# Pairs with one quarter in seven products: another order of quarters and products, another source for the second bank's copy, and a later start of the embedding weights

## The chip, the cores and the metric

The kernel runs on one core of a Trainium2 chip, as one program launched once. The metric is the time of one execution in microseconds (us) on the device. Engines are named as the profile names them: PE is TensorE (matmuls), DVE is VectorE, ACT is ScalarE, POOL is GpSimd, and SP is the queue that issues most loads. Each engine works through its own list of instructions in order; semaphores hold one engine back until another, or a DMA, is done.

## The reference, cut to what matters

The model is a trunk of two layers over 256 tokens of width 2048, each with a large input projection, a token mixer, a gate and an output projection; after the mixers stands a gated embedding of 256 inputs per layer. What the change touches are projections of width 2048 by 2048 and the product of the embedding with its weights, so only their forms matter:

```
# even layer: m is the mixers' output; odd layer the same with other weights
h   = h + m @ W_o                     # W_o: 2048 x 2048, stages "eo" and "oo"
# gated per-layer embedding
e   = rmsnorm(p @ W_p) * row          # row: one weight per feature, 2048
h   = h + sigmoid(h @ W_g) * e        # W_g: 2048 x 2048, stages "g0" and "g1"
# the odd layer's large projections, stages "oog", "oz" and others
y   = rmsnorm(h) @ W
```

The output is the whole trunk, 256 by 2048, in fp32.

## The kernel before

**Tiles.** A projection of 2048 features into 2048 is cut into four chunks of 512 output features. A chunk has four quarters: 512 of the 2048 input features each. The weights of a quarter are two tiles of 128x1024 in fp32. Every tile goes the same way: SP loads it (`raw`, five buffers), ACT rounds it to fp32r (`whi`, a CAST), DVE subtracts to get the rest (`wlo`), and PE multiplies tokens (also in a high and a low part, `ahl`) by high, low, high. A plain quarter has 24 matmuls of 128x512: 12 into the bank of the first 128 tokens, then 12 into the bank of the second. `whi` and `wlo` have four buffers each, so the CAST of a tile waits until PE has finished with the tile four before it. The PSUM banks come from pools of three (`mm`), three (`mx`) and two (`st`).

**Stages.** In `eo`, `g0` and `oo` the first two chunks are done plainly, eight quarters in the order of a list in `project_two`; then `seven` does the last two chunks as a pair. `seven` is also called by the odd layer's projections `oog` and `oz`. In a pair, some of the four quarters (`kqs`) are done for both chunks at once by a scheme with seven products (numbered 1 to 7, as in Strassen's method) in place of eight. A product has six matmuls per quarter. Four pairs have one quarter in seven products: those of `eo`, `g0` and `oo`, and the first of `oog`. Three pairs (in `oog` and `oz`) have two.

**Banks of a pair.** A and F hold the first chunk's two halves of tokens, E and B the second's. Product 1 goes into A; then ACT copies A to F and, with the sign turned, A to B (lines 334 and 335). Products 5, 6 and 7 are added up in B, 2 in A, 4 in F, and the other one into E. After 5 and after 6 ACT keeps a copy of B in SBUF (`keep`, line 316); after 7 DVE subtracts B from the copy kept after 5. The remaining quarters are plain: the first chunk's into A and F (call them a), the second's into E and B (call them b). Sums of weight tiles (line 304) are made by DVE in the tiles `ch` and `raw` in place.

**Consumers.** `seven` is a generator: it yields a finished half chunk, and its caller queues what follows. In `eo` and `oo` that is `out_proj`: DVE adds the bank to the residual (line 586, `hq`), transposes it in blocks (549, `w`), and sends it to DRAM and back in another layout (`across`), where it returns as `r`; ACT and DVE split `r` into the next stage's `ahl`. In `g0` it is `ple_gate`: a tanh, a product with the embedding `pl`, a sum into `hq`, and then the same way round (`to_features`, line 557 for the scaled reading of `r` on ACT). Steps of such work are run by `pump`, which is called between the two halves of a plain quarter and at some places of `seven`. Where an instruction lands in its engine's list is then set by a scheduler: weight CASTs and subtractions, copies of banks and the like have raised priorities.

**Embedding weights.** `row` (line 529) loads two tiles of 128x1024 by two DMAs that POOL issues (line 533), one row of weights spread over all partitions; `ple_gain` (line 537) multiplies the eight tiles `pl` by them on DVE (line 541), in eight steps that `pump` runs. They are started when the first half chunk of `eo` is handed out, and drained when `eo` is through.

**Names.** In the orders below a number behind a name tells one buffer from another: in the pair of `eo`, bank A is `mm_3425`, F `mm_3426`, B `mm_3427` and E `mx_3424` before, and A `mm_3421`, F `mm_3422`, B `mm_3423` and E `mx_3420` after.

Of the kernel before, what the change touches and what calls it, by code (L numbers as in the profile page):

```python
# [15 lines left out]
AF = mybir.ActivationFunctionType  # L16
ALU = mybir.AluOpType
# [5 lines left out]
KT = D // P  # L23
EPS = 1e-6
RSQRT_MAGIC = 0x5F3759DF


_PRM = [
# [15 lines left out]
def trunk(ctx: ExitStack, tc: tile.TileContext, a, out):  # L44
    nc = tc.nc
    v, s, gp, te, sy = nc.vector, nc.scalar, nc.gpsimd, nc.tensor, nc.sync
# [17 lines left out]
    def start(lane, gen):  # L64
        lanes.setdefault(lane, []).append(gen)
# [9 lines left out]
    def pump():  # L75
        with ExitStack() as behind:
            for ins in last.values():
                behind.enter_context(tc.issue_after(ins))
            for lane in list(lanes):
                step(lane)  # L80

    def drain(*which):
        for lane in which:
            while step(lane):
                pass
# [135 lines left out]
    def product(o, stat, parts, first=False, end=False):  # L221

        n = 2 * len(parts)
        for k in range(n):
            xh, xl = (x[k] for x in stat)
            wh, wl = (x[:, (k % 2) * 512:(k % 2 + 1) * 512] for x in parts[k // 2])
            for i, (x, y) in enumerate(((xh, wh), (xh, wl), (xl, wh))):
                with ExitStack() as behind:
                    if k + i == 0:
                        behind.enter_context(tc.issue_after(last["pe"]))  # L230
                    last["pe"] = te.matmul(o, x, y, start=(first and k + i == 0), stop=(end and k == n - 1 and i == 2),  # L231
                                           skip_group_check=True).ins
# [4 lines left out]
    def plain(w, j, kq, act, ps, first=(False, False), end=False):  # L237

        parts = load_weights(w[4 * j + kq])
        for hf in range(2):  # L240
            product(ps[hf], stationary(act, (2 * kq, 2 * kq + 1), hf), parts, first[hf], end)
            if hf == 0:
                pump()
# [35 lines left out]
        keep(d, (2, 4))  # L279
        yield  # L280

    def seven(w, j, act, qs, kqs, room, part, home=None):

        def src(b, side, kq):
            return block(w[4 * (j + b) + kq], side * 1024, 1024)

        def load(tile_of, b, side):
            tiles = []
            for kq in kqs:
                t = tile_of()  # L290
                sy.dma_start(out=t, in_=src(b, side, kq))
                tiles.append(t)
            return tiles

        def ring():
            return wp.tile([P, 1024], F32, name="raw", tag="raw", bufs=5)

        def split(tiles):
            return [split_weights(t) for t in tiles]

        def add(x, y):
            with tc.high_priority(offset=400):
                for xi, yi in zip(x, y):
                    v.tensor_tensor(out=xi, in0=xi, in1=yi, op=ALU.add)

        def add_loaded(x):
            for xi, kq in zip(x, kqs):
                gp.dma_start(out=xi, in_=src(1, 0, kq), accum_op=ALU.add)

        def soon(out, in0, in1, op):  # L310
            with tc.high_priority(offset=450):
                v.tensor_tensor(out=out, in0=in0, in1=in1, op=op)

        def keep(out, bank):
            with tc.high_priority(offset=450):
                s.copy(out, bank)

        def quadrant(side, hf):
            return stationary(act, [2 * kq + side for kq in kqs], hf)

        def combo(n):
            return [[t for kq in kqs for t in qs[n, kq][x]] for x in range(2)]

        two = len(kqs) == 2
        rest = [kq for kq in range(4) if kq not in kqs]
        E = px.tile([P, 512], F32, name="mx", tag="mx")
        A, F, B = (pm.tile([P, 512], F32, name="mm", tag="mm") for _ in range(3))
        b5, g = part(), part()
        X = load(room, 0, 0)
        product(A, quadrant(0, 0), split(X), True)  # L330
        if two:
            add_loaded(X)
        with tc.high_priority(offset=450):
            s.copy(F, A)
            s.activation(B, A, AF.Copy, scale=-1.0)  # L335
            if home is not None:
                s.copy(E, home)
        Y = load(room, 1, 1)
        product(E, combo(4), split(Y), home is None)
        if not two:  # L340
            W = load(ring, 1, 0)
            add(Y, W)
            add(W, X)
        plain(w, j, rest[0], act, (A, F))
        product(B, combo(1), split(X if two else W))
        add(X, Y)
        if two:
            add_loaded(Y)
        keep(b5, B)
        if not two:  # L350
            plain(w, j, rest[1], act, (A, F))
            product(B, combo(2), split(X))
            keep(g, B)
        pump()
        Z = load(ring, 0, 1)
        product(A, quadrant(1, 0), split(Z))
        if not two:
            add(X, Z)
        plain(w, j, rest[-1], act, (A, F))
        yield 0, 0, A  # L360
        if two:
            product(B, combo(2), split(X))
            add(X, Z)
            keep(g, B)
            product(F, quadrant(1, 1), split(X), end=True)
            pump()
        product(B, combo(3), split(Y))
        soon(b5, B, b5, ALU.subtract)
        if not two:
            product(F, quadrant(1, 1), split(X), end=True)  # L370
        soon(b5, F, b5, ALU.subtract)
        pump()
        yield 0, 1, b5
        for kq in rest:
            plain(w, j + 1, kq, act, (E, B), end=(kq == 3))
        if home is None:
            soon(g, E, g, ALU.add)
            yield 1, 0, g
        else:
            soon(home, E, g, ALU.add)  # L380
            yield 1, 0, None
        yield 1, 1, B
# [145 lines left out]
    def row(pool, tag, bufs, i):  # L528

        halves = []  # L530
        for b in range(2):
            t = pool.tile([P, 1024], F32, name="row", tag=tag, bufs=bufs)
            gp.dma_start(out=t, in_=a["rows"][i, b * 1024:(b + 1) * 1024].partition_broadcast(P))
            halves.append(t)
        return halves

    def ple_gain(pls, rows):
        yield
        for g in range(4):
            for pl in pls[g]:  # L540
                v.tensor_tensor(out=pl, in0=pl, in1=rows[g // 2][:, (g % 2) * 512:(g % 2 + 1) * 512], op=ALU.mult)
                yield
# [49 lines left out]
    def ple_gate(hq, parts, pls, rp, hss, gain, lane, more):  # L592

        nxt = {}
        for c, hf, src in parts:
            th = tp.tile([P, 512], F32, name="th", tag="th")
            h = hq[c][:, hf]
            s.activation(th, src, AF.Tanh, scale=0.5)
            v.scalar_tensor_tensor(th, th, 1.0, pls[c][hf], op0=ALU.add, op1=ALU.mult)
            v.scalar_tensor_tensor(h, th, rp[:, hf:hf + 1], h, op0=ALU.mult, op1=ALU.add)  # L600
            if not hf:
                continue
            start(f"{lane}{c}", to_features(hq[c], c, nxt, gain, lane, more))
            step(f"{lane}{c}")
            for hf in range(2):
                squared(hq[c][:, hf], hss[:, c, hf:hf + 1])
        return nxt

    def small(n, name, rows=P):
# [8 lines left out]
    pls = embed(a["pw"], None, lambda: p0.tile([P, 512], F32, name="pl", tag="pl"),  # L618
                lambda: sy.dma_start(out=prm, in_=a["prm"]))
# [82 lines left out]
    def gate_tok(w, j, act, u):  # L702
# [7 lines left out]
    mx, e0, e1, lb, omb, sp, ez, z2, pol, sp8, spm8 = (small(8, n) for n in (  # L710
        "mx", "e0", "e1", "lb", "omb", "sp", "ez", "z2", "pol", "sp8", "spm8"))
# [44 lines left out]
    if True:  # L756
        ew = a["ew"]
        fs, qs, ks, xcs = {}, {}, {}, {}
# [339 lines left out]
    def mixed():  # L1098
        for c, hf, src in two_and_seven(a["eo"], y, ready(y, "fm"), (ap, "ahl"), in_e0):
            if hf == 0 and c in (1, 2):  # L1100
                load_hq(c + 1, last["hop"])
            if (c, hf) == (0, 0):
                m0_scope.close()
                pe0.append(l0.enter_context(tc.tile_pool(name="e0", bufs=1)))
                start("pg", ple_gain(pls, row(pe0[0], "row", 2, 0)))
            yield c, hf, src

    def pieces(tile):
# [5 lines left out]

    pe0 = []
    act = out_proj(hq, mixed(), "fe")
    drain("pg")
    e0 = pe0[0]

    gr = e0.tile([P, KT, 16], F32, name="gr")  # L1120
    sy.dma_start(out=gr, in_=a["ogf"])
# [45 lines left out]
    with tc.tile_pool(name="m1", bufs=2) as m1:  # L1167
# [47 lines left out]
        li, xf, ab, Bc, Mx = (t8(n) for n in ("li", "xf", "ab", "Bc", "Mx"))  # L1215
# [465 lines left out]
```

## Time and profile before

| | us |
|---|---|
| median of three runs | 1029.18 |
| lowest and highest of them | 1028.33, 1034.85 |
| the profiled execution, its own time | 1026.88 |
| its span in the trace | 1025.1 |
| PE busy in the span | 1012.5 |
| DVE busy | 823.2 |
| ACT busy | 649.9 |
| POOL busy | 105.5 |
| start of the pair in `eo` | 343.4 |
| start of the pair in `g0` | 429.2 |
| start of the pair with one quarter in `oog` | 661.7 |
| start of the pair in `oo` | 885.2 |

The page of the profile gives busy times over the span; the prediction reads the page's totals and then single stretches of the trace: the waits of an engine, the chain of work that ended last, and each engine's instructions in order of time. A row of such a timeline reads: start, duration, engine, line, operation, out<-in, how many in a row, and in brackets how long the engine had been idle before and what released it. PE's matmuls overlap: one lasts 0.39 us and the next begins 0.23 us after its start.

### The profile page before, as it was taken

Reading aid. Unit: us, or ns where it says so; the run is one execution under the profiler, and the core shown is the slowest. Engines: PE = TensorE matmul, PEld = TensorE weight load, DVE = VectorE, ACT = ScalarE, POOL = GpSimd, SP = SyncE. Lnnn points to the kernel's source line nnn. Section 1 sums busy time; section 2 is a strip of 40 time slices with the busy share of each in tenths; the row PEclk is TensorE's granted clock in tenths of the full one; section 3 lists DMA queues with packets and bytes.
Section 4 is the critical chain, followed back from the end, with each engine's and each line's share of the span. In section 5 each row is a group of like instructions: output and inputs, shape, how many; then the busy total and the mean of one; then the engine's idle time right before and its main releaser. Section 6 shows DMA issues by size and latency. Waiting matters only on the chain.

```text
span 1025.1 us, 14489 instructions
## 1 busy us (share of the span) xinstructions
PE 1012.5 (99%) x5170; PEld 840.3 (82%) x5170; DVE 823.2 (80%) x1208; ACT 649.9 (63%) x933; POOL 105.5 (10%) x190
## 2 busy tenths in 40 slices
PE   9999999999999999999999999999999999999996
PEld 8888888888888888878888888888888888888885
DVE  7858968969686997788559997779889997976783
ACT  7675554686974555576457876766676777554652
POOL 0111101011112121021011100000011111112000
PEclk9999999999999999999999999999999999999999
DMA  9987756567689798579688755377879888689652
GB/s 363 332 248 227 221 176 199 173 199 231 229 262 295 278 313 252 179 262 311 215 293 248 232 184 189 124 229 206 257 191 283 219 285 317 197 266 304 191 184 83
DMA packets 69672, 242.14 MB, mean 236 GB/s; under 512 B 9024, under 2 KB 10432, under 8 KB 69600
## 3 DMA queue, kind: packets, MB, share of 16 engines
q1 hardware_dynamic: 54720, 193.36, 57.0%
q0 software_dynamic: 14448, 47.33, 16.6%
q8 instruction: 40, 0.66, 0.2%
q10 hardware_dynamic: 432, 0.52, 0.1%
q14 instruction: 32, 0.26, 0.1%
HBM read 221.26 MB, written 19.92 MB: 235 GB/s over the span
## 4 chain that ended last, share of the span: by engine, by line
PE 95%; ACT 2%; DVE 1%; issue 1%; DMA 1%; POOL 0%; ACTq 0%
PE mm L231 21%; PE mm L207 17%; PE mm L209 17%; PE mm L208 17%; PE mx L231 6%; PE mx L209 4%; PE mx L208 3%; PE mx L207 3%; PE mm L502 1%; PE mx L502 1%; PE mm L1506 1%; PE mm L1505 1%; PE mm L1507 1%; PE nu L1315 1%; DMA r<-dfg 1%
## 5 line engine op out<-in xcount | busy, mean ns | idle before, releaser
L136 DVE TENSOR_TENSOR wlo<-raw,whi 128x1024 fp32r<-128x1024 f32 (+1 forms) x317 | 381.4, 1213 | 127.7 <-ACT whi L135 119.9
L135 ACT CAST whi<-raw 128x1024 fp32r<-128x1024 f32 (+1 forms) x317 | 331.0, 1048 | 224.8 <-PE mm L209 108.8
L207 PE MATMUL mm<-whi,ahl 128*128 128x512 f32 x768 | 300.2, 391 | 0.0
L208 PE MATMUL mm<-wlo,ahl 128*128 128x512 f32 x768 | 299.0, 389 | 0.0
L209 PE MATMUL mm<-whi,ahl 128*128 128x512 f32 x768 | 298.9, 389 | 0.0
L231 PE MATMUL mm<-whi,ahl 128*128 128x512 f32 x552 | 178.7, 390 | 1.0 <-ACT mm L335 0.9
L207 PEld LDWEIGHTS mm<-whi,ahl 128*128 128x128 f32 x768 | 144.2, 188 | 30.2 <-issue 0.4
L209 PEld LDWEIGHTS mm<-whi,ahl 128*128 128x128 f32 x768 | 144.2, 188 | 30.1
L208 PEld LDWEIGHTS mm<-wlo,ahl 128*128 128x128 f32 x768 | 144.2, 188 | 29.3
L231 PEld LDWEIGHTS mm<-whi,ahl 128*128 128x128 f32 x552 | 103.6, 188 | 24.2 <-ACT mm L335 2.3
L231 PE MATMUL mm<-wlo,ahl 128*128 128x512 f32 x276 | 107.5, 389 | 0.0
L218 DVE TENSOR_TENSOR wlo<-ch,whi 128x1024 fp32r<-128x1024 f32 x56 | 67.5, 1222 | 11.0 <-ACT whi L217 9.4
L217 ACT CAST whi<-ch 128x1024 fp32r<-128x1024 f32 x56 | 58.3, 1052 | 15.2 <-PE mm L231 7.2
L207 PE MATMUL mx<-whi,ahl 128*128 128x512 f32 x160 | 62.2, 389 | 0.0
L208 PE MATMUL mx<-wlo,ahl 128*128 128x512 f32 x160 | 62.2, 389 | 0.0
L209 PE MATMUL mx<-whi,ahl 128*128 128x512 f32 x160 | 62.2, 389 | 0.0
L231 PEld LDWEIGHTS mm<-wlo,ahl 128*128 128x128 f32 x276 | 51.8, 188 | 10.7
L231 PE MATMUL mx<-whi,ahl 128*128 128x512 f32 x144 | 47.3, 389 | 0.0
L231 PE MATMUL mm<-whi,q 128*128 128x512 f32 x120 | 40.5, 390 | 0.0
L208 PEld LDWEIGHTS mx<-wlo,ahl 128*128 128x128 f32 x160 | 30.0, 188 | 6.3
L209 PEld LDWEIGHTS mx<-whi,ahl 128*128 128x128 f32 x160 | 30.0, 188 | 6.2
L207 PEld LDWEIGHTS mx<-whi,ahl 128*128 128x128 f32 x160 | 30.0, 188 | 6.2
(377 smaller groups left out, 1230.7 us busy)
## 6 DMA issues: line engine op xcount, KB each, us to landing
raw<-in_ew_dram SPq DMA_DIRECT2D x64, 512.0 KB, 4.9
raw<-in_g_dram SPq DMA_DIRECT2D x62, 512.0 KB, 4.7
raw<-in_oqk_dram SPq DMA_DIRECT2D x32, 512.0 KB, 4.5
raw<-in_ov_dram SPq DMA_DIRECT2D x32, 512.0 KB, 4.3
raw<-in_eo_dram SPq DMA_DIRECT2D x30, 512.0 KB, 5.3
raw<-in_oo_dram SPq DMA_DIRECT2D x30, 512.0 KB, 5.2
raw<-in_oog_dram SPq DMA_DIRECT2D x24, 512.0 KB, 4.2
raw<-in_oz_dram SPq DMA_DIRECT2D x20, 512.0 KB, 5.1
```

The lines of the kernel that those rows point to most:

```text
L135: last["act"] = s.copy(h, r).ins
L136: last["dve"] = v.tensor_tensor(out=l, in0=r, in1=h.bitcast(F32), op=ALU.subtract).ins
L207: te.matmul(ps[hf], xh, wh, start=(k == 0), stop=False)
L208: te.matmul(ps[hf], xh, wl, start=False, stop=False)
L209: last["pe"] = te.matmul(ps[hf], xl, wh, start=False, stop=(k == KT - 1)).ins
L217: last["act"] = s.copy(hi, r).ins
L218: last["dve"] = v.tensor_tensor(out=lo, in0=r, in1=hi.bitcast(F32), op=ALU.subtract).ins
L231: last["pe"] = te.matmul(o, x, y, start=(first and k + i == 0), stop=(end and k == n - 1 and i == 2), skip_group_check=True).ins
L502: last["pe"] = te.matmul(ps[hf][:, o:o + w_], tokens(pact[x], k, hf), (hi, lo)[y][:, k * 512 + o:k * 512 + o + w_], start=(n == mine[0]), ...
L1315: te.matmul(ps[:, 0:n], x[:, i, o:o + P], y[:, b, i], start=(b == 0 and x is sh and y is vh), stop=(b == hf and y is vl))
L1505: te.matmul(o, xh, wh, start=(k == 0), stop=False)
L1506: te.matmul(o, xh, wl, start=False, stop=False)
```

## The change

It has three parts.

- The order of quarters and products in a pair is now a string of letters. For a pair with one quarter in seven products the order was, in these letters, `a5a6.2aA74.Fbbb`, and is now `a5a6.7b2.4aAFbb` (digits: products; a, b: plain quarters; a point: `pump`; A, F: the half chunk is handed out). So product 7 comes right behind 6, one of the second chunk's quarters comes ahead of 2 and 4, and both halves of the first chunk are handed out together with two quarters left in place of three. Pairs with two quarters keep their order but for the place of a `pump` and of a sum of weight tiles.
- B is copied from F, with the sign turned, and no longer from A.
- The two loads and eight products of the embedding weights are started when `eo` is through, and drained in the loop of `ple_gate`, ahead of the first use.

```diff
+ORDERS = {1: "a5a6.7b2.4aAFbb", 2: "a5.2aA64.7F.bb"}
...
         with tc.high_priority(offset=450):
             s.copy(F, A)
-            s.activation(B, A, AF.Copy, scale=-1.0)
+            s.activation(B, F, AF.Copy, scale=-1.0)
...
-        plain(w, j, rest[0], act, (A, F))
-        product(B, combo(1), split(X if two else W))
-        add(X, Y)
...
-        if not two:
-            plain(w, j, rest[1], act, (A, F))
-            product(B, combo(2), split(X))
-            keep(g, B)
-        pump()
-        Z = load(ring, 0, 1)
-        product(A, quadrant(1, 0), split(Z))
...
+        rows = [list(rest), list(rest)]
+        did = set()
+        for op in order or ORDERS[len(kqs)]:
+            if op in "ab":
+                b = "ab".index(op)
+                kq = rows[b].pop(0)
+                plain(w, j + b, kq, act, ((A, F), (E, B))[b], end=not rows[b])
...
+            elif op == "6":
+                product(B, combo(2), split(X))
+                keep(g, B)
...
+            elif op == "7":
+                product(B, combo(3), split(Y))
+                soon(b5, B, b5, ALU.subtract)
...
         for c, hf, src in parts:
+            drain("pg")
             th = tp.tile([P, 512], F32, name="th", tag="th")
...
-                start("pg", ple_gain(pls, row(pe0[0], "row", 2, 0)))
...
-    drain("pg")
     e0 = pe0[0]
+    start("pg", ple_gain(pls, row(e0, "row", 2, 0)))
```

Three places of the engines' lists show what it moves. The first is PE in the pair of `eo`, from the start of product 6; `q4` are the combined tokens of a product, `ahl` plain tokens. Before, product 6 goes into bank B and then product 2 into bank A:

```order
L231 MATMUL mm_3427<-whi_3544,q4_3148 128x512 [waits Activation_49]
L231 MATMUL mm_3427<-wlo_3545,q4_3148 128x512 [waits DVE_49]
L231 MATMUL mm_3427<-whi_3544,q4_3148 128x512 x2
L231 MATMUL mm_3427<-wlo_3545,q4_3148 128x512
L231 MATMUL mm_3427<-whi_3544,q4_3148 128x512
L231 MATMUL mm_3425<-whi_3558,ahl_2791 128x512 [waits Activation_49]
L231 MATMUL mm_3425<-wlo_3559,ahl_2791 128x512 [waits DVE_49]
```

After, in the same place:

```order
L232 MATMUL mm_3423<-whi_3538,q4_3148 128x512 [waits Activation_49]
L232 MATMUL mm_3423<-wlo_3539,q4_3148 128x512 [waits DVE_49]
L232 MATMUL mm_3423<-whi_3538,q4_3148 128x512 x2
L232 MATMUL mm_3423<-wlo_3539,q4_3148 128x512
L232 MATMUL mm_3423<-whi_3538,q4_3148 128x512
L232 MATMUL mm_3423<-whi_3549,q4_3096 128x512 [waits Activation_49]
L232 MATMUL mm_3423<-wlo_3550,q4_3096 128x512 [waits DVE_49]
L232 MATMUL mm_3423<-whi_3549,q4_3096 128x512 x2
L232 MATMUL mm_3423<-wlo_3550,q4_3096 128x512
L232 MATMUL mm_3423<-whi_3549,q4_3096 128x512
L232 MATMUL mx_3420<-whi_3561,ahl_2981 128x512
```

Product 7 now follows 6 in the same bank, and its first matmul waits for ACT, whose `keep` reads that bank in between.

The second place is DVE at the end of `project_two` in `eo`; `wlo_3375` and `wlo_3381` before (`wlo_3371` and `wlo_3377` after) are the weights of its last quarter. Before:

```order
L136 TENSOR_TENSOR wlo_3319<-raw_3317,whi_3318 128x1024 [waits DMAHW2_49,Activation_49]
L136 TENSOR_TENSOR wlo_3325<-raw_3323,whi_3324 128x1024 [waits DMAHW3_49,Activation_49]
L136 TENSOR_TENSOR wlo_3375<-raw_3373,whi_3374 128x1024 [waits DMAHW4_49,Activation_49]
L136 TENSOR_TENSOR wlo_3381<-raw_3379,whi_3380 128x1024 [waits DMAHW5_49,Activation_49]
L586 TENSOR_TENSOR hq_3057<-mm_3061,hq_3057 128x512 [waits DMASW3_49,PE_49]
```

After:

```order
L137 TENSOR_TENSOR wlo_3319<-raw_3317,whi_3318 128x1024 [waits DMAHW2_49,Activation_49]
L137 TENSOR_TENSOR wlo_3325<-raw_3323,whi_3324 128x1024 [waits DMAHW3_49,Activation_49]
L545 TENSOR_TENSOR pl_219<-pl_219,row_3777 128x512 [waits DMASW6_49]
L545 TENSOR_TENSOR pl_227<-pl_227,row_3777 128x512
L137 TENSOR_TENSOR wlo_3371<-raw_3369,whi_3370 128x1024 [waits DMAHW4_49,Activation_49]
L137 TENSOR_TENSOR wlo_3377<-raw_3375,whi_3376 128x1024 [waits DMAHW5_49,Activation_49]
L590 TENSOR_TENSOR hq_3057<-mm_3061,hq_3057 128x512 [waits DMASW3_49,PE_49]
```

Though the code starts the embedding weights later, two of their eight products now stand ahead of those two subtractions, and the first of them waits for a DMA: the second of the two row loads. The other six stand in `project_two` of `g0`; before, all eight stood in the pair of `eo`. On POOL the two row loads stand where they stood.

The third place is ACT in `project_two` of `oo`; `hq_8152` is a residual tile that comes back from DRAM, and `mx_8249` the bank E of the coming pair, which starts from it (line 337 before). `whi_8089` and `whi_8095` are the weights of quarter (1,2). Before:

```order
L135 CAST whi_8039<-raw_8038 128x1024 [waits DMAHW2_49,DVE_49,PE_49]
L698 ACTIVATE xr_8056<-r_7829,prm_84 128x256 [waits DMASW6_49,DMASW7_49,DMASW5_49,DMASW0_49]
L698 ACTIVATE xr_8056<-r_7829,prm_84 128x256
L698 ACTIVATE xr_8062<-r_7829,prm_84 128x256 [waits DVE_49]
L149 CAST ahl_8059<-xr_8056 128x2x256 [waits Activation_49]
L698 ACTIVATE xr_8062<-r_7829,prm_84 128x256
L432 ACTIVATE sq_8070,pss_7824<-pl_7798 128x512
L337 COPY mx_8249<-hq_8152 128x512 [waits DMASW6_49]
L135 CAST whi_8089<-raw_8088 128x1024 [waits DMAHW3_49,PE_49]
L135 CAST whi_8095<-raw_8094 128x1024 [waits DMAHW4_49,PE_49]
L149 CAST ahl_8065<-xr_8062 128x2x256 [waits Activation_49]
```

After:

```order
L136 CAST whi_8039<-raw_8038 128x1024 [waits DMAHW2_49,DVE_49,PE_49]
L338 COPY mx_8249<-hq_8152 128x512 [waits DMASW6_49]
L703 ACTIVATE xr_8056<-r_7829,prm_84 128x256 [waits DMASW7_49,DMASW5_49,DMASW0_49]
L703 ACTIVATE xr_8056<-r_7829,prm_84 128x256
L703 ACTIVATE xr_8062<-r_7829,prm_84 128x256 [waits DVE_49]
L150 CAST ahl_8059<-xr_8056 128x2x256 [waits Activation_49]
L703 ACTIVATE xr_8062<-r_7829,prm_84 128x256
L436 ACTIVATE sq_8070,pss_7824<-pl_7798 128x512
L136 CAST whi_8089<-raw_8088 128x1024 [waits DMAHW3_49,DVE_49,PE_49]
L150 CAST ahl_8065<-xr_8062 128x2x256 [waits Activation_49]
L136 CAST whi_8095<-raw_8094 128x1024 [waits DMAHW4_49,DVE_49,PE_49]
```

The copy that waits for the DMA of `hq_8152` has moved ahead of six instructions which stood before it, and one CAST of tokens now stands between the two weight CASTs.

More of the change, by code (lines that the diff above doesn't have):

```diff
@@ L280, in combos, with seven @@
         yield
-    def seven(w, j, act, qs, kqs, room, part, home=None):
+    def seven(w, j, act, qs, kqs, room, part, home=None, order=None):
         def src(b, side, kq):
@@ L322, in combo @@
             return [[t for kq in kqs for t in qs[n, kq][x]] for x in range(2)]
-        two = len(kqs) == 2
+        acc = len(kqs) == 2
         rest = [kq for kq in range(4) if kq not in kqs]
@@ L330, in seven @@
         product(A, quadrant(0, 0), split(X), True)
-        if two:
+        if acc:
             add_loaded(X)
@@ L339, in seven @@
         product(E, combo(4), split(Y), home is None)
-        if not two:
+        W = X
+        if not acc:
             W = load(ring, 1, 0)
@@ L343, in seven @@
             add(W, X)
-        plain(w, j, rest[0], act, (A, F))
-        product(B, combo(1), split(X if two else W))
-        add(X, Y)
[L347 to L350, printed above, removed]
-            plain(w, j, rest[1], act, (A, F))
-            product(B, combo(2), split(X))
-            keep(g, B)
-        pump()
-        Z = load(ring, 0, 1)
-        product(A, quadrant(1, 0), split(Z))
[L357 to L375, printed above, removed]
+        rows = [list(rest), list(rest)]
[5 more added lines that the diff above has]
+                plain(w, j + b, kq, act, ((A, F), (E, B))[b], end=not rows[b])
+            elif op == "5":
+                product(B, combo(1), split(W))
+                add(X, Y)
+                if acc:
+                    add_loaded(Y)
+                keep(b5, B)
+            elif op == "6":
+                product(B, combo(2), split(X))
+                keep(g, B)
+            elif op == "2":
+                Z = load(ring, 0, 1)
+                product(A, quadrant(1, 0), split(Z))
+            elif op == "4":
+                product(F, quadrant(1, 1), split(X))
+            elif op == "7":
+                product(B, combo(3), split(Y))
+                soon(b5, B, b5, ALU.subtract)
+            elif op == ".":
+                pump()
+            elif op == "A":
+                yield 0, 0, A
+            elif op == "F":
+                soon(b5, F, b5, ALU.subtract)
+                yield 0, 1, b5
+            did.add(op)
+            if op in "26" and {"2", "6"} <= did:
+                add(X, Z)
         if home is None:
```

## The prediction

> **What bounds the kernel now.** I read the page's totals first, then PE's waits, then the chain of work, then single timelines around the pairs. Of the page: the span, the busy times, the chain by engine.
>
> ```profile
> span 1025.1 us, 14489 instructions
> PE 1012.5 (99%) x5170; PEld 840.3 (82%) x5170; DVE 823.2 (80%) x1208; ACT 649.9 (63%) x933; POOL 105.5 (10%) x190
> PE 95%; ACT 2%; DVE 1%; issue 1%; DMA 1%; POOL 0%; ACTq 0%
> ```
>
> PE is busy for 99% of the span, so the change, which leaves the number of matmuls alone, can only win what PE loses in waits. There is little of that, but what is newly lost counts in full. PE's waits at the pairs, by who ended them (total, times, longest):
>
> ```profile
> PE mx L231 <- DVE wlo L136: 1.3, 2, 0.7
> PE mm L231 <- ACT mm L335: 0.9, 1, 0.9
> ```
>
> The second is the copy of A to B, line 335. PE's timeline where it happens in `oog`, and a piece of the chain that gives PE's pace:
>
> ```profile
> 664.18 0.39 PE L231 MATMUL mx<-whi,q 128*128 128x512 f32 x1
> 665.51 0.50 PE L231 MATMUL mm<-whi,ahl 128*128 128x512 f32 x1 [0.95 <-ACT mm L335]
> 665.85 0.39 PE L231 MATMUL mm<-wlo,ahl 128*128 128x512 f32 x1
> ...
> 460.36 2.72 PE mm L231 x12
> ```
>
> Twelve matmuls take 2.72 us, 0.227 each from start to start. Across the wait it was 665.51 − 664.18 = 1.33: 1.10 lost. The next start follows after 0.34, so each wait costs 0.11 more: 1.21.
>
> **The change part by part.** *Copy from F.* The chain there, and the same copy's piece in `g0`:
>
> ```profile
> 431.64 0.50 ACT mm L335
> ...
> 664.00 0.60 ACT whi L217
> ...
> 664.87 0.60 ACT mm L335
> ```
>
> In `oog` a CAST stood between the two copies, and PE's first plain matmul into A needed both, since both read A. Now only the first does, and the second has until product 5, some 5 us later. In `oog` this wins the 1.21. In `g0` its 0.50 is on the chain, less the 0.16 that a pause has between 0.23 and 0.39 anyway, some 0.3, and 0.1 for the slow second start: 0.4. In `eo` and `oo` no such wait shows. Gain 1.6, between 0 and that.
>
> *Product 7 behind product 6.* Both add to bank B, and ACT's `keep` reads B between them. ACT and PE at the end of product 6 in the pair of `eo` before:
>
> ```profile
> 358.64 1.06 ACT L135 CAST whi<-raw 128x1024 fp32r<-128x1024 f32 x1 [0.30 <-PE mm L231]
> 360.00 0.59 ACT L316 COPY pr<-mm 128x512 f32<-128x512 f32 x1 [0.30 <-PE mm L231]
> ...
> 359.57 0.39 PE L231 MATMUL mm<-whi,q 128*128 128x512 f32 x1
> 359.80 0.39 PE L231 MATMUL mm<-whi,ahl 128*128 128x512 f32 x1
> ```
>
> The copy starts 0.43 after the start of the last matmul and ends at 360.59; PE then needs some 0.04 to go on. Before, PE went on at 359.80 in another bank. After, product 7 starts at 360.63: 0.83 lost, with the slow second start 0.94. In the new order a weight CAST stands ahead of the copy as it did before, and the row shows it over 0.30 before the copy can start. Four pairs: 3.8. From below it could be 0; from above the copy would stand behind a CAST that starts late, 1.05 more each, so 8.0. I take the row of the same copy, 3.8. In the pairs with two quarters the order of products stays.
>
> *The quarter b ahead of 2 and 4.* In `g0` the two waits for `wlo` go back to the chain:
>
> ```profile
> 445.08 5.64 DMA r<-dfg
> ...
> 450.88 1.31 ACT xr L557 x3
> ...
> 455.33 0.08 DVE wlo L136
> ```
>
> ACT stood in its list at the reading of `r`, which landed at 450.72, and the weight CASTs queued behind it came late. In the new order the tiles of b are CAST ahead of that reading, and the next quarter's tiles are wanted some 5 us later. The two waits, 1.3 idle, go: PE's start to start adds 0.39 − 0.23 = 0.16 to each, and 0.11 behind each: gain 1.8. Bounds 0 and 1.8. What could be late next is DVE's subtraction of B after 7, ahead of b's second half in B; it has 12 matmuls, 2.72, for itself (0.7) and a `wlo` of 1.2 ahead of it.
>
> *Handing out A and F together.* The consumers get A 9 us and F 5 us later, but two quarters, 10.9 us, of this pair and four quarters of the next stage's weights lie ahead of their first use. Cost 0; if that cover is gone, the transfer's 5.6 us from the row above. SP issues the same loads in the new order of tiles, each some buffers ahead of its CAST; PE's and ACT's waits name none of them in a pair, so 0 as well, with one load's place, a product of 1.4, as the upper end.
>
> *The embedding weights.* POOL's issues stay where they were. Two multiplies on DVE now stand ahead of the `wlo` of `eo`'s quarter (1,3) and wait for the second row load. When POOL issued the two loads, and what their landing took (first alone, both, and of all six such loads min/median/max):
>
> ```profile
> 325.89 1.09 POOL L533 DMA_DIRECT2D row<-in_rows_dram  x2 [13.30 <-ACT ahl L149]
> ...
> row<-in_rows_dram POOLq DMA_DIRECT2D x1, 512.0 KB, 8.6
> ...
> row<-in_rows_dram POOLq DMA_DIRECT2D x2, 512.0 KB, 9.6
> ...
> DMA to landing us min/median/max: 6.0/7.9/10.6
> ```
>
> The second is issued at 326.44 and lands 10.6 later (twice 9.6, less 8.6), at 337.04. DVE and PE there before, and a multiply of that kind:
>
> ```profile
> 327.02 2.58 DVE L136 TENSOR_TENSOR wlo<-raw,whi 128x1024 fp32r<-128x1024 f32 x2 [0.31 <-ACT whi L135]
> 332.46 1.22 DVE L136 TENSOR_TENSOR wlo<-raw,whi 128x1024 fp32r<-128x1024 f32 x1 [2.85 <-ACT whi L135]
> ...
> 335.41 0.69 DVE L586 TENSOR_TENSOR hq<-mm,hq 128x512 f32<-128x512 f32 x1
> ...
> 337.85 1.23 DVE L218 TENSOR_TENSOR wlo<-ch,whi 128x1024 fp32r<-128x1024 f32 x1 [1.00 <-ACT whi L217]
> ...
> 344.18 2.35 DVE L136 TENSOR_TENSOR wlo<-raw,whi 128x1024 fp32r<-128x1024 f32 x2
> ...
> 357.05 1.29 DVE L541 TENSOR_TENSOR pl<-pl,row 128x512 f32<-128x512 f32 x2
> ...
> 337.93 0.39 PE L207 MATMUL mx<-whi,ahl 128*128 128x512 f32 x1
> ...
> 346.09 0.46 PE L231 MATMUL mm<-whi,ahl 128*128 128x512 f32 x1
> ```
>
> DVE is done with the multiplies at 337.04 + 1.29 = 338.33, with the first `wlo` at 339.55. PE wants it with its second matmul of the quarter, 337.93 + 0.23 = 338.16: 1.43 lost, with the slow start 1.5. The second `wlo` is done at 340.7. Behind it DVE had, from 335.41 to the end of the first `wlo` of the pair's first plain quarter at 345.40, 9.0 us of work and 1.00 idle. Now it has that at 349.7; PE, 1.5 late, wants it at 346.09 + 0.23 + 1.5 = 347.8: 1.9 lost, 2.0 with the slow start. Together 3.5. Then DVE catches up, since the multiplies that filled it in the pair (0.65 each, six of them) have gone to `g0`, where it has idle time. In sum PE loses what the landing takes beyond 7.2 us: 0 at the shortest landing of 6.0; 6.7 if it were 13.9, the longest of a POOL load below.
>
> The Trainium skill (DMA: Bandwidth & Descriptors, "Anatomy of one DMA — SWDGE") puts such a DMA at 2.0 us plus its bytes over 436 per ns, an estimate of 3.2 us for 512 KB. By that the row would be there at 329.6 and this term would be 0. The trace has 6.0 to 10.6, so the measurement decides.
>
> *ACT in `oo`.* The copy of the residual into bank E waits for a DMA, and now stands ahead of six instructions. ACT, DVE and PE there before; of ACT's six the first group and the last:
>
> ```profile
> 859.52 1.30 ACT L698 ACTIVATE xr<-r,prm 128x256 f32<-128x256 f32 x3
> ...
> 862.17 0.18 ACT L432 ACTIVATION_READ_ACCUMULATOR sq<-pl 128x1 f32 x1
> 864.90 0.59 ACT L337 COPY mx<-hq 128x512 f32<-128x512 f32 x1 [2.55 <-DMA hq<-dh]
> 865.42 1.99 ACT L135 CAST whi<-raw 128x1024 fp32r<-128x1024 f32 x2
> ...
> 850.41 1.16 POOL L1417 DMA_DIRECT2D hq<-dh  x2 [1.36 <-DMA r<-ducn]
> ...
> 866.50 2.36 DVE L136 TENSOR_TENSOR wlo<-raw,whi 128x1024 fp32r<-128x1024 f32 x2 [3.82 <-ACT whi L135]
> ...
> 868.91 0.39 PE L207 MATMUL mx<-whi,ahl 128*128 128x512 f32 x1
> ```
>
> The six take 862.35 − 859.52 = 2.83. Behind the copy they put the CASTs from 865.42 to 868.25, and the first `wlo` from 867.70 to 870.55. PE wants it at 868.91 + 0.23 = 869.14: 1.4 lost, 0.1 for the slow start. Between the two CASTs stands one of tokens now (0.5), by which the second `wlo` comes 0.4 late. Together 1.9. Bounds: 0 if the load lands 2.6 us sooner (the six then cost ACT nothing, as before), and 2.8, all that was moved.
>
> *Sum.* −1.6 + 3.8 − 1.8 + 3.5 + 1.9 = +5.8. Against the profiled execution's 1026.88 (2.3 below the median of the runs shown, 1029.18) that is 1032.7; against the median 1035.0.
>
> **The rivals.** *The loads land in time.* If both land some us earlier than in this execution, the two queue waits are hidden, and 3.8 − 3.4 = +0.4 is left: 1029.6. The six row loads' median of 7.9 speaks for it; the other loads on the queues at that place, which do not change, against. *Only the gains.* If `keep` is hidden as well (another CAST order on ACT), −3.4: 1025.8. Against it stands that both products use one bank. *Slower by over 1%: the row comes late.* About 1% is what a measurement of this kernel can tell from no change, 10.3 us. PE loses us for us what the second row takes beyond 7.2; with the other terms at +2.3 it passes +10.3 when the landing takes over 15.2 us. The trace's longest POOL load, 13.9 (the second `hq` load above, issued at 850.99 and waited for until 864.90), gives 2.3 + 6.7 = +9.0, 1038.2; 16 us gives 1040.3. *Slower by over 1%: the clock.* If each of the some seven new waits had the clock halved for one quarter, a quarter of 24 matmuls, 5.44 us, would take 5.44 more, and one such quarter on top of +5.8 gives 1040.4, all seven 1073. The granted clock (the number ahead of the DMA share) across and behind the longest wait of before speaks against it:
>
> ```profile
> 663.00:666.00 3.00, 2.05 (x9) 1.40 (x9) 3.00 (x4) 3.00 (x5) 0.00 (x0) 1.00 0.51 165
> 666.00:669.00 3.00, 3.00 (x18) 2.55 (x17) 2.56 (x3) 0.43 (x1) 0.00 (x0) 1.00 0.80 243
> ```
>
> It stayed at 1.00 after 0.95 idle. The Trainium skill (TensorE: Matmul & The Clock Gate, "A second HAM failure mode: psum-queue depth-cycling") tells of a kernel whose small pauses at changes of PSUM banks made the clock swing between half and full; by that rule this rival would come true. The two rows show no such swing.
>
> **How the numbers follow.** Forecast (+5.8, parts of it smaller or larger by 2 or 3): 0.58. Loads in time: 0.22. Only the gains: 0.08. Row very late: 0.07. Clock: 0.05. The likeliest gives 1035.0. The range goes from 1027, between only the gains and loads in time, to 1040, where both slow rivals begin; some 0.06 is left out below and 0.10 above. Faster by over 1% would be below 1018.9, more than PE's waits hold: 0.01. Slower by over 1%, above 1039.5: the two last rivals less the row's part below it, and the forecast with 8.0 for the handover: 0.10. Within: 0.89.
>
> **What would show it.** In the profile after: four waits of PE's `mm` for ACT's `keep` of 0.6 to 0.7 idle each, one in each pair with one quarter (the handover); a group of multiplies on DVE near 330 to 338 whose idle time ahead is ended by the DMA of `row`, and PE's waits for `wlo` near 338 and 347; ACT's copy from `hq` near 865 ahead of the reading of `r`, and PE waiting for `wlo` near 869; no wait for the copy to B and none for `wlo` in the pair of `g0`. I am wrong if the second row lands within 7 us, if the copies of B are further from PE's path than the timeline says, or if a wait stands in a pair that I counted at nothing.

## The result and the profile after

| | before | after |
|---|---|---|
| median, 22 runs each, us | 1028.78 | 1035.08 |
| lowest and highest, us | 1026.16, 1034.85 | 1031.20, 1036.78 |
| profiled execution, us | 1026.88 | 1035.23 |
| its span, us | 1025.1 | 1033.5 |

The ratio of after to before is 1.0054, with a 95% interval of 1.0042 to 1.0067. On 1028.78 that is 5.6 us slower, between 4.3 and 6.9; the two medians as they stand lie 6.3 apart, inside that interval. The two profiled executions lie further apart, by 8.35 us. One execution below is left out of its ratio: one of the kernel with three edits and the old order of the pairs took 1270.47 us, at a mean granted clock of 0.752.

The page of the kernel after: its span, its busy times, and the chain of work that ended last by engine.

```profile
span 1033.5 us, 14486 instructions
...
PE 1015.4 (98%) x5170; PEld 840.6 (81%) x5170; DVE 824.0 (80%) x1208; ACT 650.9 (63%) x933; POOL 105.2 (10%) x190
...
PE 90%; DMA 4%; ACT 1%; DVE 1%; issue 1%; POOL 1%; ACTq 0%; DVEq 0%; POOLq 0%
```

PE has as many matmuls as before; its share of the chain fell from 95% to 90%, and DMA's rose from 1% to 4%. PE's waits after (total, times, longest; a further one of 0.8, `st` for PE's own sequencer at the kernel's start, is in every trace):

```profile
PE mx L208 <- ACT whi L136: 2.9, 1, 2.9
PE mm L232 <- ACT pr L317: 2.7, 4, 0.7
PE mx L209 <- DVE wlo L137: 2.0, 2, 1.3
PE mm L232 <- DVE wlo L137: 1.4, 1, 1.4
```

The two waits of before, for line 335 and for `wlo` in the pair of `g0`, are not among them. The second row is the handover from product 6 to 7, once in each pair with one quarter. ACT and PE at it in `eo`:

```profile
362.00 1.06 ACT L136 CAST whi<-raw 128x1024 fp32r<-128x1024 f32 x1 [0.30 <-PE mm L232]
363.35 0.58 ACT L317 COPY pr<-mm 128x512 f32<-128x512 f32 x1 [0.30 <-PE mm L232]
...
362.93 0.39 PE L232 MATMUL mm<-whi,q 128*128 128x512 f32 x1
363.99 0.51 PE L232 MATMUL mm<-whi,q 128*128 128x512 f32 x1 [0.68 <-ACT pr L317]
```

The copy again starts 0.42 behind the start of the last matmul of product 6, and product 7 starts 1.06 behind it. DVE and PE around the wait for the row in `eo`:

```profile
327.19 2.58 DVE L137 TENSOR_TENSOR wlo<-raw,whi 128x1024 fp32r<-128x1024 f32 x2 [0.31 <-ACT whi L136]
337.25 1.29 DVE L545 TENSOR_TENSOR pl<-pl,row 128x512 f32<-128x512 f32 x2 [7.48 <-DMA row<-in_rows_dram]
338.46 2.35 DVE L137 TENSOR_TENSOR wlo<-raw,whi 128x1024 fp32r<-128x1024 f32 x2
...
348.38 2.35 DVE L137 TENSOR_TENSOR wlo<-raw,whi 128x1024 fp32r<-128x1024 f32 x2
...
339.74 0.50 PE L209 MATMUL mx<-wlo,ahl 128*128 128x512 f32 x1 [1.25 <-DVE wlo L137]
...
347.84 0.39 PE L232 MATMUL mm<-whi,ahl 128*128 128x512 f32 x1
349.65 0.50 PE L232 MATMUL mm<-wlo,ahl 128*128 128x512 f32 x1 [1.42 <-DVE wlo L137]
```

DVE stood for 7.48 us with weight subtractions behind it in its list. PE waited 1.25 for the first of them, and DVE was still behind ten microseconds later, when PE waited a second time. Last, ACT and PE in `oo`, and the same stretch by threes of microseconds (after the span of a window: its length, the busy times of PE, PEld, DVE, ACT and POOL, then the granted clock of PE, the DMA share and GB/s):

```profile
861.24 1.06 ACT L136 CAST whi<-raw 128x1024 fp32r<-128x1024 f32 x1 [0.30 <-PE mx L210]
870.67 0.59 ACT L338 COPY mx<-hq 128x512 f32<-128x512 f32 x1 [8.37 <-DMA hq<-dh]
...
873.93 1.03 ACT L136 CAST whi<-raw 128x1024 fp32r<-128x1024 f32 x1
...
875.39 1.04 ACT L136 CAST whi<-raw 128x1024 fp32r<-128x1024 f32 x1
...
871.70 0.39 PE L210 MATMUL mm<-whi,ahl 128*128 128x512 f32 x1
875.01 0.50 PE L208 MATMUL mx<-whi,ahl 128*128 128x512 f32 x1 [2.93 <-ACT whi L136]
876.27 0.79 PE L209 MATMUL mx<-wlo,ahl 128*128 128x512 f32 x1 [0.76 <-DVE wlo L137]
876.87 0.63 PE L210 MATMUL mx<-whi,ahl 128*128 128x512 f32 x1
877.29 0.63 PE L208 MATMUL mx<-whi,ahl 128*128 128x512 f32 x1
```

```profile
872.00:875.00 3.00, 0.08 (x1) 0.00 (x0) 0.70 (x2) 3.00 (x8) 0.00 (x0) 1.00 0.00 0
875.00:878.00 3.00, 2.23 (x5) 1.62 (x6) 3.00 (x4) 3.00 (x6) 0.00 (x0) 0.70 0.24 48
878.00:881.00 3.00, 3.00 (x11) 2.35 (x11) 3.00 (x4) 0.94 (x1) 0.00 (x0) 0.73 0.84 279
881.00:884.00 3.00, 3.00 (x15) 2.48 (x14) 2.53 (x4) 1.68 (x2) 0.00 (x0) 1.00 0.86 240
```

ACT stood for 8.37 us, where before it had stood for 2.55 with the six other instructions already done. PE paused for 2.93, did one matmul, paused for 0.76, and then its matmuls started 0.42 to 0.43 apart in place of 0.23, up to 879.4, while the granted clock was 0.70 and 0.73 in the mean of two windows. The load of `hq` took 16.6 us from its issue, the maximum here:

```profile
DMA to landing us min/median/max: 2.9/8.4/16.6
```

Both kernels have 5170 matmuls, so the start of the k-th can be compared between the two traces. The differences that come up at each place, worked out that way (for the four pairs from the rows of `eo` above):

| term | forecast | measured |
|---|---|---|
| B copied from F (`g0`, `oog`) | −1.6 | −0.36 − 1.23 = −1.6 |
| b ahead of 2 and 4 (`g0`) | −1.8 | −1.9 |
| product 7 behind 6, four pairs | +3.8 | 4 x (1.06 − 0.23 + 0.11) = +3.8 |
| multiplies that wait for the row (`eo`) | +3.5 | 1.59 + 1.60 = +3.2 |
| copy that waits for `hq` (`oo`) | +1.9 | 3.09 + 2.73 = +5.8 |
| sum | +5.8 | +9.3 |

The last matmul starts 9.7 us later; the span grew by 8.4 only, since the stretch behind the last matmul was 8.5 us after and 9.8 before.

### The profile page after: what moved, and what is told of

It is laid out like the page before. It is cut to its first block, busy times and chain, and to the rows that moved or that the text cites. A ratio compares the mean times of both kernels' runs of the same rounds, so it can differ in the third digit from the quotient of the medians.

```text
span 1033.5 us, 14486 instructions
## 1 busy us (share of the span) xinstructions
PE 1015.4 (98%) x5170; PEld 840.6 (81%) x5170; DVE 824.0 (80%) x1208; ACT 650.9 (63%) x933; POOL 105.2 (10%) x190
## 3 DMA queue, kind: packets, MB, share of 16 engines
q0 software_dynamic: 14448, 47.33, 16.6%
## 4 chain that ended last, share of the span: by engine, by line
PE 90%; DMA 4%; ACT 1%; DVE 1%; issue 1%; POOL 1%; ACTq 0%; DVEq 0%; POOLq 0%
PE mm L232 21%; PE mm L208 16%; PE mm L209 16%; PE mm L210 16%; PE mx L232 5%; PE mx L209 3%; PE mx L210 3%; PE mx L208 3%; DMA hq<-dh 2%; DMA ducn<-w 1%; DMA row<-in_rows_dram 1%; PE nu L1319 1%; PE mm L1510 1%; PE mm L1509 1%; PE mm L1511 1%
```

## The experiments

Each kernel's ratio is to the kernel before, timed in the same sitting. A difference between two kernels "by the ratios" carries the uncertainty of both: an estimate from their intervals is 1.7 to 2.8 us. So the traces show where time went, and the ratios alone rarely settle a single term.

### One place of `pump` in the other string

By the lists that are generated it was not the new string for one quarter, the copy from F or the embedding weights that moved ACT's copy in `oo`. With each of them put back alone or together it stayed ahead of the six instructions; with the `pump` of the string for two quarters put back it returned, and the POOL loads with it.

```diff
-ORDERS = {1: "a5a6.7b2.4aAFbb", 2: "a5.2aA64.7F.bb"}
+ORDERS = {1: "a5a6.7b2.4aAFbb", 2: "a5.2aA64.7.Fbb"}
```

> The changed kernel with one letter of the other string moved: in a pair with two quarters the pump stands ahead of the handing out of F again, as before the change. By the order this alone puts ACT's copy from hq in oo behind the six instructions again, and POOL's row loads ahead of the first hq load. Theory (the queue place made PE's waits near 872 to 879, 5.8 us in the trace of the changed kernel): no wait of PE in project_two of oo, and about 5.5 us less than the changed kernel, near 1029.5. Rival 1 (the term is only what was forecast, 1.9, and the rest is a late landing that comes anyway): a wait of 2 to 4 us stays there, near 1033. Rival 2 (the slow matmuls near 877 come from something else than the long wait): they stay.

Median 1030.60, ratio to before 1.0029 (1.0015 to 1.0044). PE's waits in its trace:

```profile
PE mm L232 <- ACT pr L317: 2.7, 4, 0.7
PE mm L232 <- DVE wlo L137: 1.4, 1, 1.4
...
PE mx L209 <- DVE wlo L137: 0.2, 1, 0.2
```

No wait in `oo` is left, and no slow matmuls: the granted clock is 1.00 from 866 to 878. So the `pump`'s place made both; since it moves POOL's loads too, the next experiment holds back ACT's copy alone. By the ratios it is worth 1.0054 − 1.0029, 2.6 us, and not 5.5; each ratio is uncertain by 1.3 us or more.

### ACT's copy alone held back

```diff
             if home is not None:
-                s.copy(E, home)
+                with tc.issue_after(last["act"]):
+                    s.copy(E, home)
```

> The changed kernel with one thing undone in oo: ACT's copy from hq held behind the pair's first weight CAST; POOL's loads keep their new order, so the hq load still lands late. Theory (the place in ACT's list is what costs, not the load's landing by itself): no wait near 870 and no slow matmuls behind it, some 5.5 us less than the changed kernel, near 1029.5. Rival (the late landing holds PE in another way, at product 4 of the pair): a wait of 1 us or more near 890.

Median 1028.97, ratio 1.0022 (1.0011 to 1.0032). PE's waits:

```profile
PE mm L232 <- ACT pr L317: 2.7, 4, 0.7
PE mm L232 <- DVE wlo L137: 1.4, 1, 1.4
PE mx L209 <- DVE wlo L137: 1.1, 1, 1.1
```

These three are those of the handover and of `eo`. POOL's loads stood in the new order here and the longest `hq` load took 16.8 us, but nobody waited for it. It is the place in ACT's list that lets the landing cost PE anything; the late landing by itself costs nothing. By the ratios 3.3 us, with 5.5 expected.

### The embedding products held in `g0`

```diff
         for g in range(4):
             for pl in pls[g]:
-                v.tensor_tensor(out=pl, in0=pl, in1=rows[g // 2][:, (g % 2) * 512:(g % 2 + 1) * 512], op=ALU.mult)
+                with tc.issue_after(last["dve"]):
+                    v.tensor_tensor(out=pl, in0=pl, in1=rows[g // 2][:, (g % 2) * 512:(g % 2 + 1) * 512], op=ALU.mult)
```

> The changed kernel with the eight products of the embedding weights held behind the latest weight subtraction that is written ahead of them, so that all eight stand in g0. Theory: PE's waits near 338 and 348 (3.3 us) go and nothing takes their place, near 1031.8. Rival (DVE in g0 has no room for two more, or the row lands late there too): a new wait of PE for wlo in g0, no gain.

Median 1031.62, ratio 1.0031 (1.0013 to 1.0050): by the ratios 2.4 us less than the kernel after, with 3.3 expected and an uncertainty that takes it in. PE's waits:

```profile
PE mx L208 <- ACT whi L136: 3.3, 1, 3.3
PE mm L232 <- ACT pr L317: 2.7, 4, 0.7
...
PE mx L209 <- DVE wlo L137: 0.8, 1, 0.8
```

The waits in `eo` are gone; the two for `oo` stay (3.3 and 0.8, for 2.9 and 0.76 in the kernel after), and the slow matmuls behind them too. DVE in `g0` had room.

### Product 2 between 6 and 7

```diff
-ORDERS = {1: "a5a6.7b2.4aAFbb", 2: "a5.2aA64.7F.bb"}
+ORDERS = {1: "a5a6.27b.4aAFbb", 2: "a5.2aA64.7F.bb"}
```

> The changed kernel with product 2, in bank A, between 6 and 7, which both go into bank B; the quarter b still ahead of 4. Theory: the four waits of 0.7 for ACT's keep go (0.95 each with the slow second start), 3.8 us less, near 1031.3. Rival (the wait is for a busy ACT, not for the bank's handover): ACT has as many CASTs there, and waits of PE for ACT of about the same size come at product 2 or 7.

Median 1032.40, ratio 1.0032 (1.0008 to 1.0056). PE's waits:

```profile
PE mx L208 <- ACT whi L136: 2.1, 1, 2.1
PE mm L232 <- DVE wlo L137: 1.4, 1, 1.4
PE mx L209 <- DVE wlo L137: 1.1, 2, 0.8
```

The four waits for ACT's `keep` are gone, though three CASTs stand between ACT's two `keep` copies in its list as they did before this edit: it was the handover of the bank, not a busy ACT. The trace has 3.8 us less there; the median has 2.3 less by the ratios, with an uncertainty that takes in 3.8.

### The three edits together

The `pump` put back, the embedding products held in `g0`, and product 2 between 6 and 7.

```diff
-ORDERS = {1: "a5a6.7b2.4aAFbb", 2: "a5.2aA64.7F.bb"}
+ORDERS = {1: "a5a6.27b.4aAFbb", 2: "a5.2aA64.7.Fbb"}
...
+                with tc.issue_after(last["dve"]):
```

> The three edits of the other runs together: pump back, embedding products held in g0, product 2 between 6 and 7. Left of the change are the copy from F, the quarter b ahead of 4, the late start of the embedding products and both halves handed out together. Theory (the terms add up): the gains of 1.6 and 1.8 us remain, so 3.4 us faster than the kernel before, near 1025.5, ratio 0.9967. Rival (the gains are not real, or b ahead of 4 costs elsewhere): the time of the kernel before or more.

Median 1024.35, ratio 0.9965 (0.9948 to 0.9983). It is 3.6 us faster than before, between 1.7 and 5.3, with 3.4 expected; that the gains remain is shown, that the terms add up to that size only within this interval. PE's waits at the stages:

```profile
PE mx L209 <- DVE wlo L137: 0.8, 1, 0.8
PE mx L208 <- ACT whi L136: 0.3, 1, 0.3
```

Both are near 866 in `oo`. There the copy stands where it stood before, but PE is earlier and this `hq` load took 17.3 us. They cost this trace 1.6 us.

### The same, with B copied from A again

```diff
-            s.activation(B, F, AF.Copy, scale=-1.0)
+            s.activation(B, A, AF.Copy, scale=-1.0)
```

> The kernel with all three edits, with B copied from A again. Theory: the waits of the kernel before for the copy to B come back, 0.4 near 430 and 1.2 near 664, so 1.6 us slower than with all three edits, near 1026. Rival (a CAST stands between the copies either way and PE is held by something else): no difference.

Median 1025.33, ratio 0.9983 (0.9973 to 0.9993), by the ratios 1.8 slower than with F, which is not clear of their uncertainty of some 2 us. The trace is: matmuls lose 0.4 near 431 and 1.2 near 662 again, and the wait of before is back:

```profile
PE mm L232 <- ACT mm L336: 0.9, 1, 0.9
```

### The same, with the old order of the pairs

```diff
-ORDERS = {1: "a5a6.27b.4aAFbb", 2: "a5.2aA64.7.Fbb"}
+ORDERS = {1: "a5a6.2aA74.Fbbb", 2: "a5.2aA64.7.Fbb"}
```

> The kernel with all three edits, with the old order a5a6.2aA74.Fbbb for pairs with one quarter, so without the quarter b ahead of 4; the copy from F and the late embedding products stay. Theory: the two waits for wlo in the pair of g0 come back, 1.8 us slower than with all three edits, near 1026.2. Rival (they were only chance of when r landed): no difference.

Median 1025.08 of eleven executions (1025.67 with the one named above), ratio 0.9985 (0.9973 to 0.9996): 2.0 slower by the ratios, with 1.8 expected, and again not clear of the uncertainty. The trace shows one wait for `wlo` in the pair of `g0` in place of two:

```profile
PE mx L232 <- DVE wlo L137: 0.7, 1, 0.7
```

So b ahead of 4 does take the wait away, though not always whole. By the starts of the matmuls the two traces without it (before and this one) lose 1.8 and 1.2 there. Of the nine with it, six lose nothing, two lose 0.3 to 0.4, and the one with the row loaded twice 1.3. How large the wait is depends on when `r` lands.

### The three edits, and the copy in `oo` held back

The edit of the second experiment on top of the three.

> The kernel with all three edits, and ACT's copy of the residual into bank E in oo held behind the pair's first weight CAST. With all three edits PE is earlier than in the kernel before and still lost 1.5 us near 866, where that copy waits for its load. Theory: that 1.5 goes, near 1023 and under the kernel with all three edits. Rival (product 4 needs bank E at the pair's start and waits for the copy there): a new wait of PE near 884 of 0.6 or more.

Median of five executions 1022.86, ratio 0.9955 (0.9943 to 0.9967): 4.6 us faster than before, the lowest median here. By the ratios that is 1.0 less than without the copy held back, with 1.5 expected; the two intervals overlap. Its chain by engine, on the page:

```profile
PE 99%; DMA 0%; ACT 0%; issue 0%; DVE 0%; ACTq 0%; POOLq 0%
```

All of PE's waits that its trace lists:

```profile
PE mx L507 <- ACT whi L476: 0.9, 1, 0.9
PE st L98 <- PEq L1678: 0.8, 1, 0.8
```

No stage of the change is among them: the first is at the kernel's start, 5 us in. No wait came at product 4, where the copy is used.

### The row loaded twice

On the kernel of the first experiment, to make DVE's wait longer and to see the clock elsewhere.

```diff
-            gp.dma_start(out=t, in_=a["rows"][i, b * 1024:(b + 1) * 1024].partition_broadcast(P))
+            for _ in range(times):
+                gp.dma_start(out=t, in_=a["rows"][i, b * 1024:(b + 1) * 1024].partition_broadcast(P))
...
-    start("pg", ple_gain(pls, row(e0, "row", 2, 0)))
+    start("pg", ple_gain(pls, row(e0, "row", 2, 0, 2)))
```

> The kernel of the first run (pump back) with the two row loads of the even layer made twice over, one behind the other, so that DVE's wait for the row ends some 9 us later, at about 346 to 347; by the order it now stands behind the weight subtractions of quarter (1,3) and ahead of those of the pair. Theory (DVE stands in its list for the load, and PE behind it; PE's clock is halved for a while after a pause of 3 us or more, wherever it is): PE pauses near 343.6 for 4 to 6 us, and after it matmuls start 0.43 apart for some 2 to 4 us, with a granted clock under 0.9 in that stretch. Rival for the wait (DVE can go on): no pause. Rival for the clock (the slow matmuls in oo come from what else goes on there): a pause without slow matmuls.

One run, 1036.48. DVE and PE there, and the windows:

```profile
343.44 0.69 DVE L546 TENSOR_TENSOR pl<-pl,row 128x512 f32<-128x512 f32 x1 [7.81 <-DMA row<-in_rows_dram]
...
343.68 0.39 PE L232 MATMUL mm<-whi,ahl 128*128 128x512 f32 x1
347.11 0.79 PE L232 MATMUL mm<-wlo,ahl 128*128 128x512 f32 x1 [3.05 <-DVE wlo L219]
...
348.98 0.63 PE L232 MATMUL mm<-whi,ahl 128*128 128x512 f32 x1
349.41 0.63 PE L232 MATMUL mx<-whi,q 128*128 128x512 f32 x1
```

```profile
344.00:347.00 3.00, 0.07 (x1) 0.00 (x0) 3.00 (x6) 0.92 (x1) 0.00 (x0) 0.85 0.00 0
347.00:350.00 3.00, 2.89 (x7) 2.31 (x8) 3.00 (x5) 0.35 (x1) 0.29 (x1) 0.50 0.00 0
350.00:353.00 3.00, 2.60 (x7) 1.49 (x5) 3.00 (x4) 0.88 (x2) 0.36 (x2) 0.51 0.44 175
353.00:356.00 3.00, 2.56 (x11) 2.14 (x12) 3.00 (x4) 1.84 (x3) 2.80 (x5) 1.00 0.55 143
```

The row came at 343.4, 3 us sooner than expected, and PE paused for 3.05, under the 4 to 6 expected. Behind the pause matmuls start 0.43 apart up to 352, with a granted clock of 0.50. So the slow matmuls belong to the pause, in `eo` as in `oo`; this kernel ran once only.

## Why the prediction was right, and where it was not

The time was forecast at 1035.0 and is 1035.08; against before it was +5.8, and is +5.6 by the ratio, inside the range and under 1%. The last 0.1 us says nothing: the forecast stood on a median of three executions, 1029.18, which is 1028.78 with 22. The steps stand differently.

- *Copy from F, −1.6.* Right in the trace, where undoing it brings both losses back; the 1.8 by the ratios fits, but is not clear of their uncertainty.
- *Product 7 behind 6, +3.8.* Right: 0.83 for each handover and 0.11 for the slow second start, as the row of before gave. Taking the products apart took the waits away.
- *The quarter b ahead, −1.8.* Right in the trace after (−1.9); undoing it costs 1.2 in the trace and 2.0, not clear of the uncertainty, by the ratios.
- *The embedding weights, +3.5.* Right: the row landed at 337.2, forecast 337.04, and PE lost 3.2 at the two places named. Holding the products back took both losses out of the trace.
- *ACT in `oo`, +1.9.* The mechanism was right, the size was not: 5.8 in the profiled execution. The step that failed is "the first `wlo` from 867.70 to 870.55", with "2.8, all that was moved" for the upper end. It took the landing of the one execution at hand, 13.9 us, as fixed. In the eleven traces the longest `hq` load takes 13.8 to 17.5; the one of before was the shortest.
- *The same term, taken apart.* Of the price of the place alone the forecast was right. In the three traces in which the copy stands ahead of the six and PE waits (after, products held in `g0`, product 2 between), PE goes on 4.34 to 4.35 us after the copy's start; in the two in which it stands behind them and PE waits (the three edits together, row loaded twice), 1.62 after. The difference is 2.73, with 2.83 forecast. But before, the copy started at 864.90 and PE came to that quarter at 868.91, 4.01 later; after, it started at 870.67 and PE would have come at 871.93, only 1.26 later. So the copy was 2.75 later against PE, most of it the longer landing (16.6 for 13.8). With the 1.4 forecast that makes 4.15, and the two pauses measure 3.1 and 1.0. The upper end of 2.8 had no ground, since past it PE pays microsecond for microsecond. And behind a pause of that size the clock adds its part: the slow matmuls are the last 1.7 of the 5.8 (2.73 − 1.03 in the table).
- By the ratios the same term is 2.6 or 3.3 us, by the two kernels that take it away. That lies between the forecast and the trace, with some 2 us of uncertainty; why the traced executions, three of which show 5.1 to 6.2, are dearer there than the ratios say is not settled. The clocks of the single executions suggest that slow matmuls are not a matter of the traces alone: the mean granted clock was 0.996 or less in 12 of 22 executions of the kernel after, in 5 of 12 and 11 of 12 of the kernels with the products held and with product 2 between, and in none of the 24 of the two kernels that take the term away. The mark is a coarse one, since the traced execution of the kernel after had 0.997. The kernel before had 10 of 35 such executions in one sitting and 1 of 40 in the two others; what made them is not known.
- *The clock as a rival, 0.05.* It was put to every wait, and for six of those in the trace after it is wrong: behind pauses up to 1.42 us matmuls started 0.23 apart again, at a granted clock of 1.00. For the long pause in `oo` it came true. That a pause could grow that long was not worked out.
- *The pairs with two quarters.* The prediction priced no part of their string. Its one moved `pump` is what changed the lists in `oo`, a stage without such a pair. There POOL's loads moved as well, and the landing was carried over from before regardless.

That the total came out so near is luck in part: between the two traces it is 8.4 and not 5.8, and the ratios pay less in `oo` than the trace does. It is no proof of the term's size.

## What to carry to other kernels

An instruction that waits for a DMA and stands ahead of steady work in an engine's list makes that work's start the landing time of that DMA: price it by the longest landing seen, not by the one of the trace, or hold it back behind the work. Two products that add to one PSUM bank, with a copy of the bank between them, cost PE 0.94 us here, for a copy of 0.58; a product into another bank in between hid it. When a generated order is edited, compare the lists of all stages, also of those that the edit does not name: here one `pump` in another string cost more than any other single part in the trace.

## What the runs showed of the hardware

Behind a pause of PE of about 3 us the matmuls start 0.43 us apart for some 3 to 5 us, with a granted clock near 0.50, and then 0.23 again. It showed after 3.05 us idle in `eo`; in `oo` after 2.93 and 0.76 with one matmul between, and with product 2 between 6 and 7 even after 2.1 and 0.8, where the first four matmuls behind the second pause were not yet slow. It did not show after 1.42, nor after 0.59 and 0.75 with one matmul between (row loaded twice, near 877). The Trainium skill (TensorE: Matmul & The Clock Gate, Part 1, "What's actually happening") has an idle window of about 3.4 us after which the clock is halved, and a busy window of about as long until it is whole again. The traces agree with the halving and with the size of both, but not with 3.4 as a least pause: 3.05 idle, 3.44 from start to start, was enough, and so was 2.1 and 0.8 with a matmul between; where the bound lies between 1.42 and that is open. At full length the slow stretch was 4.9, longer than that window. The same page ("A second HAM failure mode: psum-queue depth-cycling") tells of small, frequent pauses at changes of PSUM banks that make the clock swing; six pauses of 0.68 to 1.42 us in the trace after, of which four are at a handover of a bank, left it at 1.00. They lie far apart, so how frequent is frequent enough is not tested here.

The landing time of one load at one place, the last of four of 512 KB issued by POOL, went from 13.8 to 17.5 us between traces of kernels that differ little.
